# A gated unit that finishes in its PSUM tile, and block differences accumulated in two PSUM banks lent by the first ring

## The chip, the cores and the metric

The kernel runs on one core of a Trainium2 chip. Its engines work from queues of their own and meet only at semaphores: TensorE (PE in the profile; PEld are its weight loads), VectorE (DVE), ScalarE (ACT), GpSimd (POOL) and SyncE (SP), which issues most transfers. Matmul results land in PSUM, eight banks of 128 partitions x 512 fp32 words; everything else lies in SBUF. GpSimd instructions in this kernel read and write SBUF alone. The metric is the device time of one execution in microseconds (us), as the median of several runs; lower is better.

## The reference, cut to what matters

One layer of a diffusion backbone over 1024 latent tokens of width 1024, after a 256-token context prefix: a bidirectional S5 state-space mixer with a gated output, then a SwiGLU feed-forward layer with 2816 hidden units, with RMS norms and adaptive shift, scale and gate around both.

```python
def out(y, h):                       # end of the S5 mixer
    y = y.reshape(h.shape).astype(h.dtype) + d_skip * h
    g = jax.nn.gelu(y)
    return g * jax.nn.sigmoid(g @ w_glu + b_glu)
...
x = x + m_l[2][:, None] * y_l
h_l = modulate(rms_norm(x, norm_ffn[i]), m_l[3][:, None], m_l[4][:, None])     # "h2"
x = x + m_l[5][:, None] * swiglu(h_l, ffn_w1[i], ffn_w3[i], ffn_w2[i])
return rms_norm(x, norm_final)
```

All arrays are fp32. The kernel reaches that accuracy with matmuls in a rounded fp32 type: each operand is split into a rounded high part and the rest, its low part, and a product takes three matmuls (high x high, high x low, low x high).

## The kernel before

The program is written in the order in which each engine runs its own instructions. No planner moves anything: generators (`glu_unit`'s `others`, `rest`, `CNT`) say in which step of one piece of work a step of another is emitted. A PSUM tile taken from a ring of `bufs` waits, on the engine that writes it first, until the earlier holder of that bank was last used.

**The gated unit.** The latent tokens are eight rows `s` of 128; the 1024 output columns are four quarters `cq`. `glu_unit(cq, s)` is one unit, 32 in all; I number them 0 to 31 in program order: units 0 to 15 run quarter by quarter over rows 0 to 3, units 16 to 31 row by row over rows 4 to 7. A unit is 24 matmuls into a PSUM tile `pz` of 256 columns (from `pe`, a ring of eight banks), then on VectorE the bias into an SBUF tile `sg` (tile name `ru`), on ScalarE the sigmoid in place, on VectorE the product with `y` and the sum with the residual row `xs`, on ScalarE a square with its row sum, written back to `pz` as a place to drop it. That square (line 1054) is the last use of the bank. Units 0 to 7 also transpose a piece of the later rows (`gt_steps`), so each takes two banks and the matmuls of unit n+4 wait for the square of unit n. GpSimd meanwhile multiplies the rows by their gate (`gate`) and, after units 1 and 5, forms the low part of the next quarter of weights (`split`, with a ScalarE copy, line 952, and the transfer `load_glu` around it).

**h2.** During units 16 to 31 the finished rows are normed and transposed: `h2s` (GpSimd) scales a row, `h2t_steps` transposes four blocks to PSUM, applies shift and scale (`kk` 0 on ScalarE, line 1110; `kk` 1 on VectorE, line 79) into the SBUF tile `tb`, copies the high part (line 1112) and subtracts it for the low part (GpSimd for `kk` 0, VectorE for `kk` 1).

**The feed-forward layer** has 22 hidden tiles of 128. Tiles 0 and 1 take the plain product (`up_plain`, n = 0 and 1 for the two halves of the tokens); each half is four quarters of 12 matmuls (`mm4`) into two `pu` banks, the first closed by a Silu on ScalarE (line 1238), the second by a VectorE product, then `gate_up` makes high and low parts. `down` follows: 16 groups of three matmuls into the `pd` ring (four banks), each added to the result by VectorE. From tile 2 on, `up` multiplies 2x2 blocks with seven products instead of eight (Strassen and Winograd's form), which needs sums and differences of the blocks of h2. These are made once, during tiles 0 and 1: for each row `t3_steps` is three VectorE operations (rows 2 and 3: GpSimd) and `t24_steps` four, the third of `t3` and the second and fourth of `t24` followed by `t_split` (a ScalarE copy, line 1154, and a GpSimd subtraction). `CNT` puts 6 of these steps into the second half of tile 0, 12 into the first half of tile 1, 7 into its second half; the rest goes into the two `down` and, for `t1_steps`, tile 2. Tile 2's first product `mm(2, 0)` stands between tile 1 and its `down`. `load2` scales and splits a tile's rows of `w2`.

Elementwise VectorE and GpSimd operations go through one helper, so the profile shows them all at line 70; tile names tell them apart: `pe`, `pu`, `pd` are PSUM, `ru`, `rxa`, `rxc`, `ra`, `r` and `c` SBUF.

Of the kernel before, what the change touches and what calls it, by code (L numbers as in the profile page):

```python
# [10 lines left out]
F32 = mybir.dt.float32  # L11
R32 = mybir.dt.float32r
I32 = mybir.dt.int32
AF = mybir.ActivationFunctionType
# [3 lines left out]
P = 128  # L18
# [19 lines left out]
def s5_ffn_kernel(tc, a, out):  # L38
    nc = tc.nc
    V, S, E, PE, SY = nc.vector, nc.scalar, nc.gpsimd, nc.tensor, nc.sync  # L40
    ctx = ExitStack()
    with ctx:
        ctx.enter_context(tc.manual_schedule())
        sb = ctx.enter_context(tc.tile_pool(name="sb", bufs=1))
        def region(tag, kb, dt=F32):
            return sb.tile([P, int(kb * 256)], dt, tag=tag, name=tag)

        def view(reg, kb, shape, parts=P):
            off = int(round(kb * 256))
            n = int(np.prod(shape))  # L50
            v = reg[:parts, off:off + n]
            if len(shape) > 1:
                names = "abcdef"[:len(shape)]
                v = v.rearrange(f"p ({' '.join(names)}) -> p {' '.join(names)}",
                                **{k: d for k, d in zip(names, shape)})
            return v
# [3 lines left out]
        RU = region("ru", 40)  # L60
# [8 lines left out]
        def tt(o, x, y, op, eng=V):  # L69
            eng.tensor_tensor(out=o, in0=x, in1=y, op=op)  # L70
# [10 lines left out]
        MUL, ADD, SUB = OP.mult, OP.add, OP.subtract  # L81
# [3 lines left out]
        def small(shape, parts=P):  # L85
            v = view(R0, pos[0], shape, parts)
            pos[0] += int(np.prod(shape)) / 256
            assert pos[0] <= 7, pos[0]
            return v
# [16 lines left out]
        ssq, ss2, rt, rtt = small([T, 4]), small([T]), small([T]), small([T])  # L106
# [16 lines left out]
        def pw(shape=(4, P)):  # L123
            return pA.tile([P] + list(shape), F32, tag="w", name="pw", bufs=3)
# [363 lines left out]
        pt = mix_rows()  # L488
# [130 lines left out]
        for hb in range(16):  # L619
# [10 lines left out]
            elif hb == 2:  # L630
                pt = mix_rows()
# [300 lines left out]
        def gt_hi(k, half, eng=S):  # L932
            pt = pe8([4, P])
            for i in range(4):
                PE.transpose(pt[:, i], Y[:, k, 4 * half + i], ident)
            if eng is S:
                S.copy(GH[half][0][:, :, k], pt)
            else:
                eng.tensor_copy(GH[half][0][:, :, k], pt)
            return pt  # L940
# [16 lines left out]
        def gh_(s):  # L957
            h_, l_ = GH[s // 4]
            return h_[:, s % 4], l_[:, s % 4]
# [4 lines left out]
        def glu_mm(cq, s, ks):  # L964

            wH, wL = (w.rearrange("p (k n) -> p k n", k=8) for w in WR[cq])
            h_, l_ = gh_(s)
            new = (cq, s) not in PZ
            if new:
                PZ[cq, s] = [pe8([256]), 0]  # L970
            pz, n = PZ[cq, s]
            for k in ks:
                PE.matmul(pz, h_[:, k], wH[:, k], start=n == 0, stop=False)
                PE.matmul(pz, h_[:, k], wL[:, k], start=False, stop=False)
                PE.matmul(pz, l_[:, k], wH[:, k], start=False, stop=n == 7)
                n += 1
            PZ[cq, s][1] = n
            return pz
# [7 lines left out]
        bglu = view(RU, 32, [D])  # L986
        SY.dma_start(bglu, a["b_glu"].to_broadcast([P, D]))
        ps_ = {}
        for i in range(10):
# [7 lines left out]
            if i >= 3:  # L997
                pt = gt_hi(order[i - 3], 0, V if i in GHV else S)
# [29 lines left out]
        GH[1] = (view(GR, 0, [4, 8, P]), view(GR, 16, [4, 8, P]))  # L1028
        WR += [(view(GR, 32 + 16 * i, [8 * 256]), view(GR, 40 + 16 * i, [8 * 256])) for i in range(3)]
        TT = [[view(GR, 32 + 16 * i + 8 * j, [4, 4, P]) for j in range(2)] for i in range(3)]  # L1030
        sg = [view(RU, 36 + i, [256]) for i in range(2)]
        ui = [0]

        def glu_unit(cq, s, *others):

            def step():
                for g in others:
                    next(g, None)

            cs_ = slice(cq * 256, cq * 256 + 256)  # L1040
            ks = order if s < 4 else range(8)
            pz = glu_mm(cq, s, ks[PZ[cq, s][1] if (cq, s) in PZ else 0:])
            step()
            o = sg[ui[0] % 2]
            ui[0] += 1
            tt(o, pz, bglu[:, cs_], ADD)
            S.activation(o, o, AF.Sigmoid)
            step()
            y = Y[:, 2 * cq:2 * cq + 2, s]
            o = o.rearrange("p (k n) -> p k n", k=2)  # L1050
            tt(o, o, y, MUL)
            tt(y, o, xs[s % 4][:, cs_].rearrange("p (k n) -> p k n", k=2), ADD)
            step()
            S.activation(pz.rearrange("p (k n) -> p k n", k=2), y, AF.Square, accum_out=ssq[:, s, cq:cq + 1])
            step()

        def gt_steps(k):
# [41 lines left out]
        def h2t_steps(s, pool, tbs, kk):  # L1099
            h_, l_ = gh_(s)  # L1100
            pt, tb, ks = pool([4, P]), tbs[kk], slice(4 * kk, 4 * kk + 4)
            for i in range(4):
                PE.transpose(pt[:, i], tb[:, i], ident)
            yield
            for i in range(4):
                k = 4 * kk + i
                if kk:
                    ts(tb[:, i], pt[:, i], mod2[:, 1, k:k + 1], MUL, mod2[:, 0, k:k + 1], ADD)
                else:
                    S.activation(tb[:, i], pt[:, i], AF.Identity, bias=mod2[:, 0, k:k + 1], scale=mod2[:, 1, k:k + 1])  # L1110
            yield
            S.copy(h_[:, ks], tb)
            yield
            tt(l_[:, ks], tb, h_[:, ks].bitcast(F32), SUB, V if kk else E)
# [17 lines left out]
        for cq in range(4):  # L1132
            for s in range(4):
                k = 4 * cq + s
# [28 lines left out]
        for u in range(16):  # L1163
            s, cq = 4 + u // 4, u % 4
            gens = []
            if u >= 2:
                j, kk = (u - 2) // 2, u % 2
# [12 lines left out]

        psF = tc.tile_pool(name="psF", bufs=1, space=bass.MemoryType.PSUM, reuse_waits="tile")
        pF = psF.__enter__()

        def pf(shape):
            return pF.tile([P] + list(shape), F32, tag="dn", name="pd", bufs=4)

        def pu_():
            return pF.tile([P, 512], F32, tag="u", name="pu", bufs=4)

        w2raw = view(RU, 32, [D])  # L1190
        tmp = [view(r, kb + 2 * i, [512]) for r, kb in ((RU, 36), (RXa, 0)) for i in range(2)]
# [20 lines left out]
        def mm4(pu, w, b, start, stop):  # L1212
            for k in range(4):
                mm3(pu, w[0][:, k], w[1][:, k], b[0][:, :, k], b[1][:, :, k], start and k == 0, stop and k == 3)
# [8 lines left out]
        def up_plain(ft, n, rest, at={}):  # L1223
            ps_ = []
            for q in range(4):
                j = (0, 2, 1, 3)[q] if n else q
                w, i = divmod(j, 2)
                if i == 0:
                    ps_.append(pu_())
                mm4(ps_[w], OP_[ft, j], bb_(i, n), i == 0, i == 1)  # L1230
                if q in at:
                    at[q]()
                if n and (ft + 1 < NPL or j < 2):
                    op_split(ft + 1, j, raw[:, j])
                for _ in range(CNT[ft][n][q]):
                    next(rest, None)
            t = tmp[n]
            S.activation(t, ps_[0], AF.Silu)
            tt(t, ps_[1], t, MUL)
            gate_up(ft, n, t)  # L1240

# [3 lines left out]
        def bb_(i, j):  # L1245
            return [t[:, :, 4 * i:4 * i + 4] for t in GH[j]]
# [11 lines left out]

        def t3_steps(s, t, eng):
            b12, b22 = (f32s(hl(x, s)) for x in (BV[6], BV[5]))  # L1260
            tt(t, b22[0], b12[0], SUB, eng)
            yield
            tt(t, t, b22[1], ADD, eng)
            yield
            tt(t, t, b12[1], SUB, eng)
            t_split(hl(BV[3], s), t, E)
            yield

        def t24_steps(s, t3, t2, t4):
            b11, b21 = (f32s(hl(x, s)) for x in BV[:2])  # L1270
            tt(t2, t3, b11[0], ADD)
            yield
            tt(t2, t2, b11[1], ADD)
            t_split(hl(BV[2], s), t2, E)
            yield
            tt(t4, t2, b21[0], SUB)
            yield
            tt(t4, t4, b21[1], SUB)
            t_split(hl(BV[4], s), t4, E)
            yield  # L1280

# [27 lines left out]
        def mm(ft, j):  # L1309
            pu = pu_()  # L1310
            mm4(pu, OP_[ft, j], BV[j], True, True)
            return pu
# [110 lines left out]
        load2(1)  # L1423
        up_plain(1, 0, rest)
        up_plain(1, 1, rest)
        pu = mm(NPL, 0)
        down([NPL - 1], False, prep(NPL))

# [4 lines left out]
        for ft in range(NPL, NFT - 1):  # L1433
            load2(ft)
            pu = up(ft, pu, {j: t1_go for j in range(4)} if ft == NPL else {})
# [64 lines left out]
```

## Time and profile before

| | |
|---|---|
| median of 3 runs | 1121.35 us (1119.0 to 1121.96) |
| the profiled execution | 1119.82 us; span of its trace 1117.6 us |
| mean granted TensorE clock | 0.961 of full |
| TensorE busy | 1005.8 us, 90% of the span |
| VectorE, GpSimd, ScalarE busy | 821.7 us, 629.6 us, 415.1 us |
| S5 mixer, up to the gated unit | to about 308 us of the span |
| gated unit and h2 | about 308 to 420 us |
| hidden tiles 0 and 1 | about 420 to 510 us |
| hidden tiles 2 to 21, final norm | about 510 us to the end |

A group row of the profile reads: line, engine, operation, out<-in by tile names, shapes, count | busy time, mean ns of one | idle time of the engine just before them and who ended it. A timeline row reads: start, duration, engine, line, operation, and in brackets the idle time before it and its releaser. A row over windows gives for each stretch its length, then each engine's busy time with its number of instructions, the granted TensorE clock (1.00 is full), the share of the transfer engines and GB/s. A matmul's shown duration overlaps the next one's; the distance between starts is what counts.

### The profile page before, as it was taken

The numbers are of one execution on the slowest core, as the hardware profiler recorded it, in microseconds if no ns is written. First come the engines' busy times: TensorE is split into PE (matmuls) and PEld (weight loads), VectorE is DVE, ScalarE is ACT, GpSimd is POOL, SyncE is SP. The second block draws the span as 40 slices with busy tenths as digits, with TensorE's granted clock in tenths as the row PEclk, the third lists the DMA queues.
The fourth block names the chain that finished last, engine by engine and source line by source line (L and its number), as shares of the span: only waits on it lengthen the run. The fifth ranks groups of instructions, "written<-read, shape, count | busy, mean of one in ns | idle before, by whom it ended". The sixth has DMA issues, their size and how long they took to land. (4 is left out here: it accounts for less than half of the span.)

```text
span 1117.6 us, 16924 instructions
## 1 busy us (share of the span) xinstructions
PE 1005.8 (90%) x6208; PEld 807.3 (72%) x6208; DVE 821.7 (74%) x1808; ACT 415.1 (37%) x870; POOL 629.6 (56%) x484
## 2 busy tenths in 40 slices
PE   4889896637969999879999999999999999999997
PEld 1556632536869997667888888888888888888885
DVE  7688989993877787988666666666666666666657
ACT  4338731625834564232222222222222222222236
POOL 4446777980382353865655555555555555555563
PEclk9989998768999999899999999999999999999999
DMA  9577778663421201101111111111111111111114
GB/s 327 212 208 152 189 247 223 160 137 99 152 76 41 75 1 59 59 15 57 57 57 56 37 35 43 57 57 57 57 57 57 57 57 57 57 57 57 40 37 150
DMA packets 54514, 103.04 MB, mean 92 GB/s; under 512 B 4384, under 2 KB 25120, under 8 KB 53408
## 3 DMA queue, kind: packets, MB, share of 16 engines
q1 hardware_dynamic: 46656, 85.57, 23.1%
q0 software_dynamic: 3456, 12.58, 6.0%
q10 hardware_dynamic: 4320, 3.81, 1.1%
q8 instruction: 49, 0.80, 0.3%
q14 instruction: 33, 0.27, 0.1%
HBM read 83.20 MB, written 6.16 MB: 80 GB/s over the span
## 5 line engine op out<-in xcount | busy, mean ns | idle before, releaser
L70 POOL TENSOR_TENSOR c<-rxc,c 128x512 fp32r<-128x512 f32 x128 | 170.3, 1345 | 184.4 <-ACT c L1154 179.4
L70 DVE TENSOR_TENSOR ru<-pd,ru 128x512 f32<-128x512 f32 x336 | 227.0, 690 | 2.6 <-PE pd L1210 2.6
L1210 PE MATMUL pu<-ra,c 128*128 128x512 f32 x432 | 168.3, 390 | 0.6 <-POOL c L70 0.6
L1209 PE MATMUL pu<-ra,c 128*128 128x512 f32 x432 | 168.2, 389 | 0.6 <-DVE ra L70 0.6
L1208 PE MATMUL pu<-ra,c 128*128 128x512 f32 x432 | 168.3, 390 | 0.3 <-ACT ra L1154 0.3
L1154 ACT CAST c<-rxc 128x512 fp32r<-128x512 f32 x128 | 76.8, 617 | 187.5 <-POOL rxc L70 107.4
L1208 PE MATMUL pd<-c 128*128 128x512 f32 x336 | 133.3, 397 | 10.9 <-DVE ru L70 10.9
L1209 PE MATMUL pd<-c 128*128 128x512 f32 x336 | 132.6, 395 | 0.0
L1210 PE MATMUL pd<-c 128*128 128x512 f32 x336 | 132.2, 394 | 0.0
L70 DVE TENSOR_TENSOR ru<-pu,ru 128x512 f32<-128x512 f32 x84 | 57.9, 689 | 86.8 <-PE pu L1210 52.0
L70 POOL TENSOR_TENSOR c<-ru,c 128x1024 fp32r<-128x1024 f32 x22 | 53.2, 2419 | 85.7 <-ACT c L952 77.1
L1210 PEld LDWEIGHTS pu<-ra,c 128*128 128x128 f32 x432 | 81.1, 188 | 18.3 <-POOL c L70 1.4
L1209 PEld LDWEIGHTS pu<-ra,c 128*128 128x128 f32 x432 | 81.1, 188 | 17.7 <-POOL c L70 0.9
L1208 PEld LDWEIGHTS pu<-ra,c 128*128 128x128 f32 x432 | 81.1, 188 | 17.5 <-ACT ra L1154 0.8
L1208 PEld LDWEIGHTS pd<-c 128*128 128x128 f32 x336 | 64.2, 191 | 26.3 <-DVE ru L70 12.9
L1210 PE MATMUL pu<-c,c 128*128 128x512 f32 x192 | 74.8, 390 | 0.2 <-POOL c L70 0.2
L1208 PE MATMUL pu<-c,c 128*128 128x512 f32 x192 | 74.9, 390 | 0.0
L1209 PE MATMUL pu<-c,c 128*128 128x512 f32 x192 | 74.7, 389 | 0.0
L1210 PEld LDWEIGHTS pd<-c 128*128 128x128 f32 x336 | 64.2, 191 | 13.6
L1209 PEld LDWEIGHTS pd<-c 128*128 128x128 f32 x336 | 64.2, 191 | 13.2
L70 DVE TENSOR_TENSOR ru<-ru,rxa 128x512 f32<-128x512 f32 (+1 forms) x62 | 62.3, 1006 | 7.4 <-ACT ru L1353 3.5
L70 POOL TENSOR_TENSOR c<-rxc,rxa 128x1024 f32<-128x1024 f32 x30 | 62.3, 2158 | 4.5 <-PE pw L602 4.5
(320 smaller groups left out, 2230.2 us busy)
## 6 DMA issues: line engine op xcount, KB each, us to landing
ru<-in_w SPq DMA_DIRECT2D x22, 512.0 KB, 3.6
c<-in_ada_w SPq DMA_DIRECT2D x40, 256.0 KB, 4.5
rxc<-in_w SPq DMA_DIRECT2D x38, 256.0 KB, 4.6
rxc<-in_w SPq DMA_DIRECT2D x19, 512.0 KB, 5.3
c<-c POOLq DMA_DIRECT2D x18, 512.0 KB, 5.4
ra<-in_ada_w SPq DMA_DIRECT2D x24, 256.0 KB, 5.6
ra<-in_ada_w SPq DMA_DIRECT2D x10, 512.0 KB, 11.0
ru<-in_xT SPq DMA_DIRECT2D x4, 1024.0 KB, 7.8
```

The costliest lines, as they stand in the source:

```text
L70: eng.tensor_tensor(out=o, in0=x, in1=y, op=op)
L1154: S.copy(o[0], x)
L1208: PE.matmul(pu, wh, bh, start=start, stop=False)
L1209: PE.matmul(pu, wh, bl, start=False, stop=False)
L1210: PE.matmul(pu, wl, bh, start=False, stop=stop)
```

## The change

1. In `glu_unit` the SBUF tiles `sg` are gone. Bias, sigmoid and product are written in place into `pz`; the sum with `xs` reads `pz` and writes `y` as before. The square goes to the same tile as before.
2. In `h2t_steps` the half `kk` 1 applies shift and scale in place in the PSUM tile of its transposes; the copy of the high part and the subtraction read that tile.
3. `t3_steps` (on VectorE) and `t24_steps` take a tile `pt` of 512 columns in PSUM. ScalarE copies the first block into it, VectorE accumulates the next block or blocks there, and the last operation of each chain reads it and writes the SBUF tile as before. These are ten new ScalarE copies.
4. The pool for tiles 0 and 1 has four `pd`, two `pu` (four before) and two `pt`. Behind tile 1's second half it is closed and one with four `pd` and four `pu` is opened.
5. In `up_plain` the Silu is emitted as soon as the first `pu` is full (after quarter 1 of half 0, quarter 2 of half 1), not behind the half.

```diff
@@ glu_unit
             pz = glu_mm(cq, s, ks[PZ[cq, s][1] if (cq, s) in PZ else 0:])
             step()
-            o = sg[ui[0] % 2]
-            ui[0] += 1
-            tt(o, pz, bglu[:, cs_], ADD)
-            S.activation(o, o, AF.Sigmoid)
+            tt(pz, pz, bglu[:, cs_], ADD)
+            S.activation(pz, pz, AF.Sigmoid)
             step()
             y = Y[:, 2 * cq:2 * cq + 2, s]
-            o = o.rearrange("p (k n) -> p k n", k=2)
+            o = pz.rearrange("p (k n) -> p k n", k=2)
             tt(o, o, y, MUL)
             tt(y, o, xs[s % 4][:, cs_].rearrange("p (k n) -> p k n", k=2), ADD)
             step()
-            S.activation(pz.rearrange("p (k n) -> p k n", k=2), y, AF.Square, accum_out=ssq[:, s, cq:cq + 1])
+            S.activation(o, y, AF.Square, accum_out=ssq[:, s, cq:cq + 1])
@@ h2t_steps
             yield
+            if kk:
+                tb = pt
             for i in range(4):
@@ the pool of tiles 0 and 1
+        NPU = [2]
         def pu_():
-            return pF.tile([P, 512], F32, tag="u", name="pu", bufs=4)
+            return pF.tile([P, 512], F32, tag="u", name="pu", bufs=NPU[0])
+
+        def pt_():
+            return pF.tile([P, 512], F32, tag="t", name="pt", bufs=2)
@@ up_plain
                 mm4(ps_[w], OP_[ft, j], bb_(i, n), i == 0, i == 1)
+                if q == 1 + n:
+                    t = tmp[n]
+                    S.activation(t, ps_[0], AF.Silu)
                 if q in at:
...
-            t = tmp[n]
-            S.activation(t, ps_[0], AF.Silu)
             tt(t, ps_[1], t, MUL)
@@ t3_steps
-            tt(t, b22[0], b12[0], SUB, eng)
-            yield
-            tt(t, t, b22[1], ADD, eng)
-            yield
-            tt(t, t, b12[1], SUB, eng)
+            a_ = t
+            if eng is V:
+                a_ = pt_()
+                S.copy(a_, b12[0])
+            tt(a_, b22[0], b12[0] if a_ is t else a_, SUB, eng)
+            yield
+            tt(a_, a_, b22[1], ADD, eng)
+            yield
+            tt(t, a_, b12[1], SUB, eng)
             t_split(hl(BV[3], s), t, E)
@@ t24_steps
-            tt(t2, t3, b11[0], ADD)
-            yield
-            tt(t2, t2, b11[1], ADD)
+            a_ = pt_()
+            S.copy(a_, b11[0])
+            tt(a_, t3, a_, ADD)
+            yield
+            tt(t2, a_, b11[1], ADD)
             t_split(hl(BV[2], s), t2, E)
             yield
-            tt(t4, t2, b21[0], SUB)
-            yield
-            tt(t4, t4, b21[1], SUB)
+            a_ = pt_()
+            S.copy(a_, b21[0])
+            tt(a_, t2, a_, SUB)
+            yield
+            tt(t4, a_, b21[1], SUB)
             t_split(hl(BV[4], s), t4, E)
@@ between tile 1 and mm(2, 0)
         up_plain(1, 1, rest)
+        psF.__exit__(None, None, None)
+        psF = tc.tile_pool(name="psG", bufs=1, space=bass.MemoryType.PSUM, reuse_waits="tile")
+        pF = psF.__enter__()
+        NPU[0] = 4
         pu = mm(NPL, 0)
```

Two places in the order of the engines' instructions. VectorE at unit 0, first before and then as changed (the first two rows lie ahead of the unit; in the next three `pe` is the unit's PSUM tile, `ru` the bias, the old SBUF tile and `y`, `c_3168` the residual row; the last row is of `gt_steps`):

```order
L70 TENSOR_TENSOR c_2975<-pe,c_2974 128x4x128 x3
L70 TENSOR_TENSOR ra<-rxc,ra 128x2048
L70 TENSOR_TENSOR ru<-pe,ru 128x256
L70 TENSOR_TENSOR ru<-ru 128x256
L70 TENSOR_TENSOR ru<-ru,c_3168 128x2x128
L70 TENSOR_TENSOR ra<-pe,ra 128x4x128
```

```order
L70 TENSOR_TENSOR c_2975<-pe,c_2974 128x4x128 x3
L70 TENSOR_TENSOR ra<-rxc,ra 128x2048
L70 TENSOR_TENSOR pe<-pe,ru 128x256 x2
L70 TENSOR_TENSOR ru<-pe,c_3168 128x2x128
L70 TENSOR_TENSOR ra<-pe,ra 128x4x128
```

Bias, product and sum keep their places (bias and product read alike now and share the row marked x2), but product and sum have one PSUM and one SBUF input where both lay in SBUF.

ScalarE in the first half of tile 1, first before and then as changed (`ru<-pu` is the Silu, `ra<-rxa` and `ra<-r_60` the copies of `t_split`, `c_4432<-ru` the copy of `gate_up`; the `pt` rows are the new copies):

```order
L952 CAST c_4432<-ru 128x1024
L1154 CAST ra<-rxa 128x512 x2
L1154 CAST ra<-r_60 128x512
L1154 CAST ra<-rxa 128x512 x2
L1238 ACTIVATE ru<-pu 128x512
L1219 CAST c_4432<-ru 128x512
```

```order
L952 CAST c_4432<-ru 128x1024
L1266 COPY pt<-ra 128x512
L1151 CAST ra<-rxa 128x512
L1234 ACTIVATE ru<-pu 128x512
L1278 COPY pt<-c_2974 128x512
L1151 CAST ra<-rxa 128x512
L1285 COPY pt<-c_2974 128x512
L1151 CAST ra<-r_60 128x512
L1278 COPY pt<-c_2974 128x512
L1151 CAST ra<-rxa 128x512
L1285 COPY pt<-c_2974 128x512
```

The Silu stands further ahead, and each new copy stands behind the `t_split` copy of the chain before it, whose input is that chain's last VectorE operation; the next chain's first VectorE operation reads what the new copy writes.

More of the change, by code (lines that the diff above doesn't have):

```diff
@@ L1030, in s5_ffn_kernel @@
         TT = [[view(GR, 32 + 16 * i + 8 * j, [4, 4, P]) for j in range(2)] for i in range(3)]
-        sg = [view(RU, 36 + i, [256]) for i in range(2)]
-        ui = [0]
         def glu_unit(cq, s, *others):
```

## Prediction

> **What bounds the kernel now.** I read the totals, then busy time by stage (PE, PEld, DVE, ACT, POOL, then the granted clock), then what TensorE waits for.
>
> ```profile
> PE 1005.8 (90%) x6208; PEld 807.3 (72%) x6208; DVE 821.7 (74%) x1808; ACT 415.1 (37%) x870; POOL 629.6 (56%) x484
> ...
> 310.22:341.77 31.55, 22.55 (x171) 21.84 (x170) 25.63 (x26) 11.64 (x27) 21.82 (x8) 0.89 0.20 68
> 341.77:420.27 78.50, 76.24 (x635) 75.23 (x634) 63.15 (x141) 38.98 (x113) 33.60 (x25) 1.00 0.13 41
> ...
> 447.26:466.08 18.82, 13.90 (x50) 10.49 (x49) 17.02 (x21) 3.80 (x7) 16.58 (x13) 0.82 0.22 80
> 466.08:491.10 25.02, 24.77 (x110) 20.19 (x109) 23.16 (x20) 7.05 (x11) 15.87 (x11) 1.00 0.07 22
> 491.10:510.54 19.44, 13.41 (x49) 10.56 (x48) 17.16 (x22) 4.02 (x7) 13.07 (x10) 0.82 0.00 0
> 527.00:1085.00 558.00, 557.58 (x2459) 461.03 (x2458) 365.72 (x518) 149.49 (x246) 313.02 (x228) 1.00 0.16 52
> ```
>
> The borders are first matmuls of stages: units 2 to 7; units 8 to 31; (tile 0 up left out); tile 0's `down`; tile 1 up with mm(2, 0); its `down`; steady tiles. In the last row TensorE is busy 557.6 of 558 us at full clock, so nothing gained on VectorE there shortens it. The room lies in the rows above: 9.0 us idle in the first, 2.3, 4.9, 0.3 and 6.0 in the next four, and a clock under 0.9 in three of them. Who ends TensorE's waits there:
>
> ```profile
> PE pd L1208 <- DVE ru L70: 10.9, 2, 6.0
> PE pe L973 <- ACT pe L1054: 9.0, 3, 6.2
> PE pe L1103 <- POOL rxa L70: 2.3, 5, 0.9
> PE pd L1103 <- DVE rxa L77: 2.2, 1, 2.2
> ```
>
> ScalarE's square at 1054 is late only because VectorE is late, so three of the four are VectorE's. The longest of them in time order (VectorE, GpSimd, TensorE):
>
> ```profile
> 326.10 3.99 DVE L70 TENSOR_TENSOR ru<-ru 128x256 f32<-128x256 f32 x1 [2.37 <-ACT ru L1047]
> 330.13 2.44 DVE L70 TENSOR_TENSOR ru<-ru,c 128x256 f32<-128x256 f32 x1
> ...
> 325.28 4.53 POOL L70 TENSOR_TENSOR ra<-rxc,ra 128x2048 fp32r<-128x2048 f32 x1 [2.76 <-ACT ra L952]
> ...
> 333.23 0.58 PE L973 MATMUL pe<-ra,c 128*128 128x256 f32 x1 [6.20 <-ACT pe L1054]
> ```
>
> The product of 256 columns ends 0.28 us behind the GpSimd instruction that began before it: it waited for it whole. Groups of 308 to 345 us, then 345 to 420, show which forms suffer:
>
> ```profile
> L70 DVE TENSOR_TENSOR ru<-ru 128x256 f32<-128x256 f32 x7 | 12.7, 1812 | 7.4 <-ACT ru L1047 7.4
> ...
> L70 DVE TENSOR_TENSOR ru<-pe,ru 128x256 f32<-128x256 f32 x7 | 2.9, 411 | 0.0
> ...
> L70 DVE TENSOR_TENSOR ru<-ru,c 128x256 f32<-128x256 f32 x24 | 18.9, 785 | 0.8
> L70 DVE TENSOR_TENSOR ru<-ru 128x256 f32<-128x256 f32 x24 | 16.3, 679 | 11.8 <-ACT ru L1047 11.8
> ```
>
> Two SBUF inputs cost 0.68 to 1.81 us on average, one PSUM input 0.41 under the same GpSimd load.
>
> **The change, part by part.** First, the price of an operation that writes PSUM (groups of the S5 mixer, where such tiles exist):
>
> ```profile
> L70 DVE TENSOR_TENSOR ltb<-ra,lta 128x256 f32<-128x256 f32 x17 | 7.2, 426 | 3.3 <-ACT ra L521 1.8 <-ACT ltb L684 1.2
> L70 DVE TENSOR_TENSOR lta<-ra,lta 128x64 f32<-128x64 f32 x96 | 21.2, 220 | 0.2
> L696 ACT COPY kt<-r 128x480 f32<-128x480 f32 x1 | 0.5, 548 | 0.0
> ```
>
> PSUM and SBUF in, PSUM out is 0.43 us at 256 columns, and with input and output in one bank (second row) no dearer in kind. I take 0.42 for product and sum; bounds 0.41 and, for the unshown in-place form at this width, twice that. A copy of 512 columns into PSUM I take at 0.57, scaled from 0.548 for 480.
>
> *Units 0 to 7.* Undisturbed, a unit costs TensorE the distance of two transposes:
>
> ```profile
> 313.18 0.60 PE L935 MATMUL pe<-r,ru 128*128 128x128 f32 x4
> 316.49 0.60 PE L935 MATMUL pe<-r,ru 128*128 128x128 f32 x4
> ...
> 341.42 0.60 PE L935 MATMUL pe<-r,ru 128*128 128x128 f32 x4
> ```
>
> 3.31 us. Units 4 to 7 took 24.93 where 13.24 would do: 11.7 lost, 9.0 waiting and the rest at half clock. VectorE's unit becomes 3 x 0.42, 0.5 for the sigmoid and 0.68 for the low part: 2.4 us, under 3.31. What is late next is a transfer that ScalarE's queue meets:
>
> ```profile
> 312.72 0.38 SPq L1019 DMA_DIRECT2D rxc<-in_w_glu  x1
> ...
> rxc<-in_w_glu SPq DMA_DIRECT2D x2, 1024.0 KB, 5.1
> ...
> L952 ACT CAST ra<-rxc 128x2048 fp32r<-128x2048 f32 x3 | 5.7, 1900 | 0.0
> ```
>
> The copy behind unit 1 (line 952) cannot start before 312.7 + 5.1 = 317.8 and takes 1.9, one of 0.6 follows, so unit 2's sigmoid starts at 320.3; its product, sum and square end at 322.2, and unit 6's matmuls need them at 316.85 + 2 x 3.31 = 323.5. The copy behind unit 5 meets a transfer that GpSimd's subtraction releases at about 325.5 (gates to 321, then the 4.53): it lands at 330.6, and ScalarE's queue stands until 332.5. Units 8 to 11 take one bank each, and unit 12 needs unit 6's square (about 335) only at 342. So nothing, with 7 us to spare. **-11.7 us**; bounds -7 (the 1.3 us margin at unit 6 gone, and at 7 too) and -11.7.
>
> *Units 16 to 31.*
>
> ```profile
> L79 DVE TENSOR_SCALAR rxa<-pe,r 128x128 f32<-128x128 f32 x24 | 8.2, 401 | 0.3
> L70 DVE TENSOR_TENSOR c<-rxa,c 128x512 fp32r<-128x512 f32 x4 | 4.4, 1102 | 0.0
> ```
>
> The 0.3 us waits of h2's transposes follow VectorE's lag (POOL's subtraction waits for ScalarE, which stands behind a late sigmoid). Over two units VectorE drops from about 6.5 us (2 x 0.42, 0.68 + 0.79 twice, four operations of 0.40, one of 1.10) and a sigmoid's wait of 0.5 to 6 x 0.42 + 1.6 + 0.69 = 4.8 and that wait, in TensorE's 2 x 3.31 = 6.6. **-1.9** of the 2.3; bounds 0 and -2.3. The 2.2 us on line 77, where unit 31's norm chain is late, goes the same way: the last four units save 0.63 each and a low part 0.4, some 2.9 us. **-2.2**, bounds -1 and -2.2.
>
> The Trainium skill, "VectorE: DVE Perf Modes", section "Rules for kernel authors", speaks against all this: for elementwise work on a matmul's output it says to copy PSUM to SBUF first if many operations follow, and the page's cycle table (its section on the TRN2 errata) has 62 more fixed cycles for a PSUM source. That would be an estimated 65 ns for each of two operations in 32 units: 4 us on VectorE, within the slack above, and a word for the rival called slower below. This trace disagrees: 411 ns with a PSUM input against 679 or more without, since GpSimd is at work beside it.
>
> *Tile 0.* Its block differences and pd groups, before:
>
> ```profile
> 454.30 0.68 DVE L70 TENSOR_TENSOR ru<-pd,ru 128x512 f32<-128x512 f32 x1
> ...
> 455.04 0.80 PE L1208 MATMUL pd<-c 128*128 128x512 f32 x1 [4.90 <-DVE ru L70]
> ...
> 437.13 1.28 ACT L1238 ACT_TABLE_LOAD   x1
> ...
> 443.26 1.13 ACT L1154 CAST c<-rxc 128x512 fp32r<-128x512 f32 x2
> ...
> 440.44 0.69 DVE L70 TENSOR_TENSOR c<-ru,c 128x512 fp32r<-128x512 f32 x1 [0.69 <-ACT c L1219]
> ```
>
> The fifth pd group waits for the first's sum, 18.0 us after the second half of the up product began (four quarters of 2.75 ahead of 447.26: 436.26). Now the Silu is early: the table load of 1.28, the Silu and the first product of some 0.6 each leave the chain ahead of `gate_up` and lie under matmuls, so `load2`'s product is done 2.6 us sooner, and behind two ScalarE copies the one into `pt` ends at 5.5 us of the half. A chain of two VectorE operations takes 0.73 + 0.69 (0.04 between them, as at 330.13); then `t_split`'s copy (0.51 to the next start, from 1.13 for two) and the new copy (0.57) with two handovers of 0.04: 1.16 in which VectorE waits if nothing else is due. So t3 ends at 7.75, the first chain of t24 at 10.3, its third operation at 12.2, the product at 12.9, the low part (two SBUF inputs, 1.4 again) at 15.0, the first pd sum at 15.7. The fifth group waits 2.0 instead of 4.9, too short for the half clock (18.82 - 11.0 - 4.9 = 2.9 us here; the waits of 4.9, 6.0 and 6.2 have it, the stages with 2.2 and less do not), and the sixth 0.65 for the one difference between. 18.82 becomes 11.0 + 2.65: **-5.2**; bounds -2 and -7.9 (no wait at all).
>
> *Tile 1.* Here the ring of two `pu` decides. T is the start of its first half. Before:
>
> ```profile
> 485.41 0.69 DVE L70 TENSOR_TENSOR ru<-pu,ru 128x512 f32<-128x512 f32 x1 [0.59 <-ACT ru L1238]
> ...
> 500.01 0.79 PE L1208 MATMUL pd<-c 128*128 128x512 f32 x1 [6.03 <-DVE ru L70]
> ...
> L70 DVE TENSOR_TENSOR rxa<-rxa,c 128x512 f32<-128x512 f32 x6 | 8.0, 1339 | 0.3
> ...
> 466.88 2.25 DVE L70 TENSOR_TENSOR ru<-ru,rxa 128x1024 f32<-128x1024 f32 x1
> ...
> 499.00:505.00 6.00, 4.99 (x12) 3.94 (x13) 4.76 (x8) 1.14 (x2) 5.19 (x4) 0.51 0.00 0
> ```
>
> 108 matmuls in 24.77 us make a quarter 2.75. The product at T+19.3 (466.08 to 485.41) emptied the second `pu` with no one waiting; TensorE ran to the fifth pd group and waited 6.0 there, then had half clock (0.51): 19.44 - 11.0 - 6.0 = 2.4 more. Now quarter 1 of the second half needs that bank at T+13.75, and behind it on TensorE stand the rest of the half, mm(2, 0) and `down`. VectorE: four pd sums to T+2.1, `load2`'s product to 4.5 (2.25 again, behind GpSimd), two ScalarE copies, t3 from 6.7 to 8.8, three ScalarE instructions, t24's first chain 10.5 to 11.9; three more chains at 1.42 + 1.16 = 2.58 to 19.6, one copy and one operation to 21.5, product to 22.2. A pair of differences thus takes 2.58 where two at 1.34 took 2.68: the gain per operation is spent on waiting for ScalarE. TensorE waits 8.4 us, loses some 1.0 at half clock (less than 2.4, since more of that state passes in the longer wait), then needs 3 x 2.75 + 2.75 + 11.0; VectorE has seven differences, two products and two low parts more (about 12 us, to T+34.5), done when `down` has just begun, so the 6.0 there is gone. End at T+45.1 against 44.46: **+0.6**; bounds -7 (the copies run ahead and the bank comes at T+15) and +6 (each chain 1 us longer).
>
> Sum: 11.7 + 1.9 + 2.2 + 5.2 - 0.6 = 20.4 off the profiled execution's 1119.8 gives 1099.4; the median lies 1.5 higher, 1100.9. I say 1100.
>
> **The rivals.** *ScalarE's chain costs more* (0.14): its copies queue behind `op_split`'s, which wait for TensorE to free a weight slot. For it: one queue holds both. Against: in the walk above the new copies' inputs are always later than those slots. At 1 us a chain +5 in tile 1 and +2 in tile 0: 1107. *The ring of two does no harm* (0.08): chains without the wait end at T+15 and tile 1 gains 7: 1093. The order shown speaks against it, since the new copy stands behind the old one. *Nothing is freed* (0.04): a VectorE operation with one SBUF input still waits for GpSimd when it also writes PSUM. Time 1120. The 0.41 with a PSUM input and the 426 above, in a kernel whose GpSimd is 56% busy, are against. *Slower* (0.05): reading and writing one PSUM bank costs double. Per pair of units 2 biases, 2 products and 4 shift-and-scales are in place; VectorE has 6.6 - 4.8 - 0.5 = 1.3 us of slack, so from 0.16 us each TensorE pays; at +0.42, 2 us in each of eight pairs, the 4.1 of the lead-in not regained, +2 and +4 in tiles 0 and 1: 1120 - 20.4 + 26 = 1125. The 220 for 64 columns in place speaks against.
>
> **How the numbers follow.** Forecast 0.69, own range 1095 to 1105. All bounds at once give 1089 and 1116; the range is 1092 to 1110, which takes in the first two rivals and the bounds that can fall together. About 0.3% is what a measurement of this kernel can tell from no change: faster 0.91, same 0.04, slower 0.05.
>
> **What would show it.** Right: units 0 to 7 at 3.31 us; `ru<-pe,c` at 0.42; no wait of line 973 on 1054; one wait of some 8 us of `pu` on VectorE in tile 1's second half and none at its `down`; about 2 us at tile 0's. Wrong: a wait for `pt`, in-place rows above 0.5 us, or a steady stage that is no longer full.

## The result and the profile after

| | before | as changed |
|---|---|---|
| median | 1121.35 us | 1101.32 us (1099.35 to 1101.53, five runs) |
| ratio of the medians | 1 | 0.9823, 95% interval 0.9806 to 0.9841 |
| profiled execution, its span | 1119.82 us, 1117.6 us | 1099.35 us, 1097.1 us |
| mean granted TensorE clock | 0.961 | 0.969 |

The change takes 20 us off, 1.8%. The totals of the changed kernel (busy time of each engine) and its stages, at the borders that the prediction used (units 2 to 7; units 8 to 31; tile 0 up; tile 0's `down`; tile 1 up with mm(2, 0); its `down`; steady tiles; in each row the span, then busy time of PE, PEld, DVE, ACT and POOL, the granted clock, and the transfers):

```profile
PE 1000.6 (91%) x6208; PEld 803.8 (73%) x6208; DVE 777.2 (71%) x1808; ACT 419.2 (38%) x880; POOL 621.8 (57%) x484
```

```profile
311.20:331.09 19.89, 19.89 (x172) 19.89 (x170) 13.59 (x26) 10.51 (x26) 19.89 (x8) 1.00 0.28 91
331.09:406.27 75.18, 75.18 (x635) 75.18 (x634) 50.42 (x146) 41.81 (x120) 33.52 (x26) 1.00 0.15 47
406.27:430.87 24.60, 24.60 (x124) 20.73 (x123) 14.50 (x36) 14.56 (x29) 10.59 (x9) 1.00 0.24 86
430.87:444.22 13.35, 11.50 (x50) 8.86 (x48) 12.30 (x19) 2.75 (x5) 9.98 (x9) 1.00 0.24 79
444.22:479.23 35.01, 26.09 (x109) 21.17 (x108) 18.99 (x26) 13.20 (x23) 22.68 (x17) 0.90 0.05 16
479.23:490.11 10.88, 10.88 (x49) 9.01 (x48) 10.34 (x16) 1.14 (x2) 6.58 (x5) 1.00 0.00 0
...
507.00:1065.00 558.00, 557.52 (x2457) 460.87 (x2456) 367.51 (x518) 149.53 (x247) 312.29 (x227) 1.00 0.16 52
```

Against the rows of before: 31.55 became 19.89 (-11.7), 78.50 became 75.18 (-3.3), 26.99 became 24.60 (-2.4), 18.82 became 13.35 (-5.5), and tile 1 with its `down`, 44.46, became 45.89 (+1.4). That sums to -21.4. The part ahead of the units was 1.0 longer in this execution (the border row that stood at 310.22 stands at 311.20), which leaves about the 20.5 between the spans. In the first three rows TensorE is now busy for the whole stretch at full clock, so no wait is left to remove there; the steady tiles are what they were. Of the long waits one is left in these stages, and it is new (TensorE's waits between 308 and 490 us, sum, count, longest):

```profile
PE pu L1209 <- DVE ru L70: 8.9, 1, 8.9
PE pd L1209 <- DVE ru L70: 1.9, 2, 1.6
```

Bias, product and sum of a unit, in the stretch of units 2 to 7 (groups by form):

```profile
L70 DVE TENSOR_TENSOR pe<-pe,ru 128x256 f32<-128x256 f32 x13 | 5.6, 427 | 5.5 <-ACT pe L1042 5.5
...
L70 DVE TENSOR_TENSOR ru<-pe,c 128x256 f32<-128x256 f32 x6 | 2.5, 424 | 0.2
```

All three take 0.42 to 0.43 us, where the product took 1.81, and GpSimd is busy beside them all through the stretch (19.89 us in the first row). The PSUM form is not quicker in itself: where GpSimd was idle in the kernel before, the product with two SBUF inputs took as little:

```profile
336.99 0.42 DVE L70 TENSOR_TENSOR ru<-ru 128x256 f32<-128x256 f32 x1 [0.51 <-ACT ru L1047]
```

### The profile page after: what moved, and what is told of

It is laid out like the page before. It is cut to its first block, busy times and chain, and to the rows that moved or that the text cites. A ratio compares the mean times of both kernels' runs of the same rounds, so it can differ in the third digit from the quotient of the medians.

```text
span 1097.1 us, 16934 instructions
## 1 busy us (share of the span) xinstructions
PE 1000.6 (91%) x6208; PEld 803.8 (73%) x6208; DVE 777.2 (71%) x1808; ACT 419.2 (38%) x880; POOL 621.8 (57%) x484
## 4 chain that ended last, share of the span: by engine, by line
PE 74%; DMA 6%; ACT 6%; DVE 6%; POOL 5%; issue 2%; ACTq 0%; SPq 0%; POOLq 0%; DVEq 0%
PE pu L1211 11%; PE pu L1210 11%; PE pu L1209 11%; PE pd L1209 7%; PE pd L1211 7%; PE pd L1210 7%; PE pw L516 3%; PE pe L974 3%; PE pe L975 3%; PE pe L973 3%; POOL c L70 3%; DVE ru L70 2%; PE prow L282 2%; DMA rxc<-in_cxy 1%; PE pm L470 1%
## 5 line engine op out<-in xcount | busy, mean ns | idle before, releaser
L70 POOL TENSOR_TENSOR c<-rxc,c 128x512 fp32r<-128x512 f32 x128 | 166.9, 1319 | 186.9 <-ACT c L1151 179.8
L1209 PE MATMUL pd<-c 128*128 128x512 f32 x336 | 131.1, 390 | 1.9 <-DVE ru L70 1.9
L1211 PE MATMUL pd<-c 128*128 128x512 f32 x336 | 130.7, 389 | 0.0
L1210 PE MATMUL pd<-c 128*128 128x512 f32 x336 | 130.7, 389 | 0.0
L1209 PEld LDWEIGHTS pd<-c 128*128 128x128 f32 x336 | 63.1, 188 | 16.1 <-DVE ru L70 3.1
L1211 PEld LDWEIGHTS pd<-c 128*128 128x128 f32 x336 | 63.1, 188 | 13.1
L1210 PEld LDWEIGHTS pd<-c 128*128 128x128 f32 x336 | 63.1, 188 | 12.9
L952 ACT CAST c<-ru 128x1024 fp32r<-128x1024 f32 x21 | 22.1, 1050 | 112.8 <-DVE ru L70 112.8
```

What stands on the lines that cost most here:

```text
L952: S.copy(hl[0], raw)
L1209: PE.matmul(pu, wh, bh, start=start, stop=False)
L1210: PE.matmul(pu, wh, bl, start=False, stop=False)
L1211: PE.matmul(pu, wl, bh, start=False, stop=stop)
```

## The experiments

Seven more kernels, and the changed kernel once more. Each is told by the same five stretches (the kernel with GpSimd's work in pieces only in its own section); tile 1 stands with mm(2, 0) and its `down`. "After" is the first profile of the changed kernel; the last rows are ratios to the kernel before, from runs on the same chip as each.

| us | before | after | units alone | tiles alone | no `pt` | ring 3 and 3 | copies ahead | ahead, no part 2 |
|---|---|---|---|---|---|---|---|---|
| units 2 to 7 | 31.55 | 19.89 | 19.88 | 32.03 | 19.88 | 19.88 | 19.88 | 19.88 |
| units 8 to 31 | 78.50 | 75.18 | 75.18 | 78.48 | 75.18 | 75.19 | 75.19 | 75.19 |
| tile 0 up | 26.99 | 24.60 | 24.60 | 26.98 | 24.59 | 24.59 | 24.59 | 24.59 |
| tile 0 down | 18.82 | 13.35 | 19.16 | 13.37 | 15.41 | 14.04 | 12.13 | 12.13 |
| tile 1 | 44.46 | 45.89 | 44.47 | 46.95 | 43.82 | 44.22 | 36.01 | 35.94 |
| ratio | 1 | 0.9823 | 0.9842 | 0.9975 | 0.9805 | 0.9808 | 0.9715 | 0.9711 |
| 95% from | | 0.9806 | 0.9812 | 0.9958 | 0.9781 | 0.9783 | 0.9689 | 0.9687 |
| to | | 0.9841 | 0.9872 | 0.9992 | 0.9830 | 0.9834 | 0.9741 | 0.9735 |

The stretches repeat to some hundredths where nothing waits, while the work ahead of the units ends up to 5 us earlier or later from one execution to the next (units 2 to 7 begin at 306 to 311 us). So a part's price is read from its stretch, and the total is the check on it.

### Is it the length of GpSimd's instructions?

The theory is that a VectorE operation with two SBUF inputs waits for the running GpSimd instruction as a whole. If so, the cure needs no PSUM: GpSimd's work in shorter pieces must do as well.

```diff
 (the kernel before; the low part of a quarter of weights, and the gates)
-            tt(hl[1], raw, hl[0].bitcast(F32), SUB, eng)
+            m = 256 if eng is E and raw.shape[-1] == 2048 else raw.shape[-1]
+            for i in range(0, raw.shape[-1], m):
+                p = slice(i, i + m)
+                tt(hl[1][:, p], raw[:, p], hl[0][:, p].bitcast(F32), SUB, eng)
...
         def gate(s, ks):
+            (one instruction for each row and 256 columns)
```

> The kernel before, with GpSimd's work during units 0 to 7 cut into instructions of 256 columns: the low part of a quarter of weights as eight instructions in place of one of 2048 columns, the gates as pieces of 256 columns; the same elements are computed, nothing of VectorE's is changed. Theory (a VectorE operation with two SBUF inputs waits for the running GpSimd instruction as a whole): no wait is longer than one piece, some 0.6 us, so the product and sum of a unit go from 1.81 and more to 0.5 to 1.0 us in the mean, TensorE's 9.0 us of waits on the square fall to 0 to 3, and the time by 6 to 12 us, 1109 to 1115. Rival (the two engines share the SBUF path element by element, so that the length of an instruction doesn't matter): the mean stays within 0.2 us of 1.81 and the time within 2 us of the kernel before, or above it by the fixed cost of the added instructions.

Measured: 1113.35 us, 6.6 under the kernel before, ratio 0.9947 (0.9925 to 0.9969). The groups of VectorE and GpSimd from 306 to 328 us, then the stretches of units 2 to 7, units 8 to 31 and tile 0 up:

```profile
L70 DVE TENSOR_TENSOR ru<-ru 128x256 f32<-128x256 f32 x6 | 4.4, 732 | 5.0 <-ACT ru L1050 5.0
...
L70 POOL TENSOR_TENSOR ru<-ru,rxa 128x256 f32<-128x256 f32 x19 | 16.4, 900 | 0.0
L70 POOL TENSOR_TENSOR ra<-rxc,ra 128x256 fp32r<-128x256 f32 x8 | 6.3, 826 | 0.0
```

```profile
308.06:327.93 19.87, 19.87 (x171) 19.87 (x169) 14.74 (x22) 10.18 (x24) 19.87 (x24) 1.00 0.16 54
327.93:410.20 82.27, 78.41 (x635) 76.88 (x634) 62.41 (x145) 40.54 (x115) 42.41 (x44) 0.98 0.16 52
410.20:438.77 28.57, 26.40 (x123) 21.92 (x122) 19.71 (x40) 14.13 (x30) 9.45 (x6) 0.94 0.17 58
```

The product went from 1.81 to 0.73 us with VectorE's program untouched, TensorE's 9.0 us of waits are gone, and units 2 to 7 take 19.87 us, as in the changed kernel. The rival (the two share the path element by element) falls. The single instructions say the same. Between 306 and 345 us, eight products and sums of the kernel before and 18 of this one start while a GpSimd instruction runs, and every one ends 0.28 to 0.29 us behind that instruction's end, whether it then took 4.15 us or 0.44. The Trainium skill, "SBUF — State Buffer", section "Who interferes with whom", states it as these rows and those of the changed units show it: an instruction of VectorE with two SBUF inputs contends with a GpSimd instruction that reads SBUF, one with at most one SBUF input doesn't (outside that engine's two-port modes).

The same profile shows what the PSUM form is better at. Eight pieces of 256 columns take 6.3 us on GpSimd where one instruction took 4.53, so the last quarter's low part comes late: TensorE waits 1.7 us for it and runs at half clock after, and units 8 to 31 give back 3.8 of the 11.7 us. The 1.6 us of the last stretch have another cause. The kernel before has the same wait of 2.2 us there (line 77), but kept its full clock, while here half clock followed it. The same stretch before, and the wait here:

```profile
420.27:447.26 26.99, 24.82 (x124) 20.65 (x123) 19.91 (x40) 14.04 (x30) 9.45 (x6) 1.00 0.18 62
```

```profile
420.81 1.48 PE L1114 MATMUL pd<-r,rxa 128*128 128x128 f32 x8 [2.17 <-DVE rxa L77]
```

### The unit alone, and the tiles alone

The kernel before with part 1 only (the unit in its PSUM tile, the diff's first part), and with parts 3 to 5 only (`pt`, the pools, the early Silu):

> The kernel before with part 1 alone: bias, sigmoid and product of a gated unit in its PSUM tile. Theory (the two-SBUF-input operations are what waits for GpSimd, in the unit itself): units 2 to 7 go from 31.55 us to 19.6 to 20.1, no wait of TensorE on the square is left, units 8 to 31 lose 1 to 2 of their 78.5 us, the 2.2 us wait on line 77 ahead of tile 0 shrinks to 0 to 1.2; the waits of 4.9 and 6.0 us at the two downs stay. In all -14 to -16 us, 1105 to 1107. Rival (the gain of units 16 to 31 and of line 77 belongs to part 2, the h2 half in PSUM): -12 us, 1109, units 8 to 31 at 78 to 78.5 and the 2.2 us wait still there.

> The kernel before with parts 3, 4 and 5 alone: block differences in two PSUM tiles, four pd, two pu, early Silu. Theory: tile 0's down goes from 18.8 to 13 to 14 us, tile 1 with mm(2, 0) and its down stays within -1 to +2 of 44.5 with one wait of 8 to 9 us on pu in the place of the 6.0 us at down; the units stay as before. In all -4 to -5.5 us, 1116 to 1117.5. Rival (these parts only do well behind a faster unit stage, since their copies queue behind late work there): within 2 us of the kernel before.

Measured: the unit alone 1101.02 us, ratio 0.9842 (0.9812 to 0.9872); the tiles alone 1117.77 us, 0.9975 (0.9958 to 0.9992). Stretches of the unit alone (units 2 to 7, 8 to 31, tile 0 up) and its waits of TensorE from 308 to 490 us:

```profile
306.20:326.08 19.88, 19.88 (x172) 19.88 (x170) 13.58 (x26) 10.51 (x26) 19.88 (x8) 1.00 0.27 91
326.08:401.26 75.18, 75.18 (x635) 75.18 (x634) 50.41 (x145) 41.43 (x118) 33.02 (x26) 1.00 0.16 48
401.26:425.86 24.60, 24.60 (x124) 20.73 (x123) 16.87 (x36) 12.46 (x26) 8.73 (x6) 1.00 0.20 67
```

```profile
PE pd L1203 <- DVE ru L70: 10.9, 2, 6.0
```

The three stretches are those of the changed kernel to 0.01 us, without part 2. So all of their 17.4 us is part 1's, and the two `down` keep their 4.9 and 6.0. The median's 18.9 less agrees with -17.0 for the five rows of the table within its interval (-14 to -21). That is more than the 14 to 16 I had expected: units 8 to 31 gave 3.3 and not 1 to 2, and the wait on line 77 is gone altogether. The rival, that part 2 has a share of it, falls. The tiles alone gave -5.45 at tile 0's `down` and +2.5 at tile 1, -2.2 us in all by the medians, where -4 to -5.5 was expected: with 0.5 lost again in the untouched units 2 to 7; the wait on `pu` was the expected one (8.9 us), but the half clock behind it lasted longer. The rival here (these parts only do well behind a faster unit stage) falls by tile 0's `down`: 13.37 us behind the old units, 13.35 behind the new. Two profiles of the changed kernel itself show how much that half clock varies with nothing changed, since it was run once more:

> The changed kernel itself, to have it on one chip beside the three below: 0.980 to 0.984 of the kernel before.

Its median was 1098.97 us, 0.9819 (0.9792 to 0.9847), the same result. After the same wait (8.92 and 8.96 us), stretches of 1 us from where TensorE resumes, in the first profile and in this one:

```profile
466.90:467.90 1.00, 1.00 (x2) 0.83 (x3) 0.37 (x1) 1.00 (x2) 0.00 (x0) 0.50 0.00 0
...
468.90:469.90 1.00, 1.00 (x4) 0.78 (x3) 0.00 (x0) 1.00 (x2) 0.82 (x2) 0.58 0.00 0
469.90:470.90 1.00, 1.00 (x6) 0.81 (x5) 0.87 (x2) 0.06 (x1) 0.94 (x1) 1.00 0.00 0
```

```profile
468.62:469.62 1.00, 0.99 (x2) 0.83 (x3) 0.37 (x1) 1.00 (x2) 0.00 (x0) 0.50 0.00 0
...
472.62:473.62 1.00, 1.00 (x4) 0.79 (x3) 1.00 (x2) 0.45 (x1) 0.00 (x0) 0.50 0.00 0
473.62:474.62 1.00, 1.00 (x6) 0.83 (x5) 0.93 (x3) 0.17 (x1) 0.75 (x1) 0.98 0.00 0
```

Half clock for 2.8 us in one, 5.0 in the other: tile 1 and its `down` took 45.89 and 46.98 us. The tiles alone had 5.0 too.

### What does `pt` bring as it stands?

The changed kernel without part 3 and without the pools of part 4, so four `pu` and four `pd` throughout:

```diff
-            a_ = pt_()
-            S.copy(a_, b11[0])
-            tt(a_, t3, a_, ADD)
+            tt(t2, t3, b11[0], ADD)
             yield
-            tt(t2, a_, b11[1], ADD)
+            tt(t2, t2, b11[1], ADD)
 (the same for the other chains; no psG)
```

> The changed kernel without part 3: the block differences in SBUF by VectorE alone as before, no copies into pt, four pu and four pd throughout; units, h2 and the early Silu as changed. Theory by the prediction's walk (the early Silu takes 2.6 us out of VectorE's chain ahead of tile 0's fifth pd group, the rest of that gain is the differences'): tile 0's down 15 to 16.5 us (13.35 as changed, 18.82 before), tile 1 with down 44 to 45 (45.9 as changed): 0 to +2 us against the changed kernel. Rival 1 (the Silu's place does nothing, since VectorE stands on the differences anyway): tile 0's down stays at 18 to 19, +3.5 to +5. Rival 2 (all of tile 0's gain is the Silu's): 13 to 13.5, -1.5 to -1.

Measured: 1097.97 us, ratio 0.9805 (0.9781 to 0.9830), beside 0.9819 for the changed kernel in the same comparison: no difference that these runs can tell. Tile 0's `down`:

```profile
429.38:444.79 15.41, 12.78 (x49) 9.62 (x48) 14.38 (x19) 2.82 (x5) 13.20 (x10) 0.89 0.20 68
```

The early Silu alone brings tile 0's `down` from 19.16 (the unit alone) to 15.41. The wait of its fifth group falls from 4.9 to 2.2 us, as the prediction's walk (its step-by-step timing) had it, though some half clock stays behind it (0.89 in the stage). `pt` brings 2.06 more there and costs 2.1 to 3.2 in tile 1 (43.82 against 45.89 and 46.98). So as it stands part 3, with its pools, pays nothing, and possibly costs 1 us.

### Ring or chain?

Two readings of the 8.9 us wait: the ring of two `pu` is too short, or VectorE comes too late because each chain of two differences waits for ScalarE. The chain, in the changed kernel, on VectorE and on ScalarE (start, duration, engine, line, operation, idle time before it and its releaser):

```profile
457.50 0.70 DVE L70 TENSOR_TENSOR pt<-rxa,pt 128x512 f32<-128x512 f32 x1 [1.18 <-ACT pt L1285]
458.30 0.69 DVE L70 TENSOR_TENSOR r<-pt,c 128x512 f32<-128x512 f32 x1
460.23 0.70 DVE L70 TENSOR_TENSOR pt<-r,pt 128x512 f32<-128x512 f32 x1 [1.24 <-ACT pt L1278]
```

```profile
448.85 0.62 ACT L1151 CAST ra<-r 128x512 fp32r<-128x512 f32 x1 [6.25 <-POOL r L70]
...
450.33 0.58 ACT L1266 COPY pt<-ra 128x512 f32<-128x512 f32 x1
...
459.02 0.62 ACT L1151 CAST ra<-r 128x512 fp32r<-128x512 f32 x1 [1.56 <-DVE r L70]
459.54 0.58 ACT L1278 COPY pt<-c 128x512 f32<-128x512 f32 x1
```

This chain takes 2.73 us (457.50 to 460.23; its neighbours take 2.66): VectorE's two operations, then ScalarE's copy of the result and only behind it the copy that the next chain starts from. Nor is that copy's input late: it is a block of h2 that was finished before tile 1 began. The first `pt` copy of tile 1 (450.33) stood behind a copy for which ScalarE had waited 6.25 us on GpSimd. The first experiment moves the copies, the second the ring.

```diff
 (copies one chain ahead: SRC lists the first block of each chain in order)
+        def fetch():
+            if SRC:
+                PT.append(pt_())
+                S.copy(PT[-1], b0(*SRC.pop(0)))
...
-            a_ = pt_()
-            S.copy(a_, b11[0])
+            a_ = PT.pop(0)
             tt(a_, t3, a_, ADD)
             yield
+            fetch()
             tt(t2, a_, b11[1], ADD)
             t_split(hl(BV[2], s), t2, E)
```

> The changed kernel with each of the new ScalarE copies issued one chain earlier, ahead of the t_split copy of the chain before, so that the next chain's first block lies in PSUM when VectorE comes. Theory (the chain VectorE - t_split copy - new copy - VectorE is what makes the 8.9 us wait in tile 1, not the ring of two itself): a chain of two operations falls from about 2.7 to 1.4 to 1.6 us on VectorE, the wait of 8.9 us in tile 1 falls under 1 us, the half clock behind it goes with it, and the waits of 1.62 and 0.23 us at tile 0's down go to about 0: tile 1 with down from 45.9 to 35.5 to 37, in all -9 to -12 us against the changed kernel, 1089 to 1092. Rival (VectorE is late in tile 1 anyway, since GpSimd's low parts and the reuse of the difference tiles set the pace, or the wait goes to down): the wait on pu shrinks by less than half or another of 4 us or more appears, -5 to 0 us, 1096 to 1101.

```diff
 (ring 3 and 3: the first pool)
-            return pF.tile([P] + list(shape), F32, tag="dn", name="pd", bufs=4)
+            return pF.tile([P] + list(shape), F32, tag="dn", name="pd", bufs=NPD[0])
...
-        NPU = [2]
+        NPU = [3]
+        NPD = [3]
...
-        NPU[0] = 4
+        NPU[0] = NPD[0] = 4
```

> The changed kernel with three pu and three pd instead of two and four in the first pool (two pt as before; four of each behind it). Theory (VectorE's late order is what costs, the ring of two only shows it): the 8.9 us wait on pu in tile 1 goes, TensorE runs on into its down, and waits 5 to 8 us there for a pd sum that stands behind the same differences on VectorE; tile 1 with down 43 to 47.5 against 45.9, tile 0's down 0 to 1 us longer: -3 to +2 us against the changed kernel. Rival (the ring of two is the cost of the change in tile 1): the wait goes and none comes in its place, -7 to -10 us.

Measured: copies ahead 1087.55 us, ratio 0.9715 (0.9689 to 0.9741); ring of three 1098.38 us, 0.9808 (0.9783 to 0.9834). Copies ahead, tile 0's `down`, tile 1 and its `down`, and TensorE's waits from 306 to 474 us:

```profile
425.67:437.80 12.13, 11.48 (x49) 8.85 (x48) 11.24 (x18) 2.95 (x5) 10.45 (x9) 1.00 0.24 86
437.80:462.93 25.13, 24.82 (x109) 20.20 (x108) 20.27 (x26) 12.77 (x22) 22.88 (x16) 1.00 0.07 22
462.93:473.81 10.88, 10.88 (x49) 9.01 (x48) 10.88 (x16) 1.15 (x2) 7.14 (x6) 1.00 0.00 0
```

```profile
PE pd L1209 <- DVE ru L70: 0.6, 2, 0.4
PE pu L1209 <- DVE ru L70: 0.3, 1, 0.3
```

With the ring still at two, the wait of 8.9 us is 0.3, and tile 1 takes 25.13 us where 24.7 is its matmuls alone. With its `down` it takes 36.0, inside the 35.5 to 37 that I expected; the time is 1.5 us under the 1089 to 1092. VectorE's chains in that run:

```profile
446.14 0.70 DVE L70 TENSOR_TENSOR pt<-rxa,pt 128x512 f32<-128x512 f32 x1
446.94 0.69 DVE L70 TENSOR_TENSOR r<-pt,c 128x512 f32<-128x512 f32 x1
447.55 0.69 DVE L70 TENSOR_TENSOR pt<-r,pt 128x512 f32<-128x512 f32 x1
```

1.41 us from one chain to the next here, between 1.4 and 1.6 elsewhere in the row. Ring of three, tile 1 and its `down`, and its waits from 431 to 489 us:

```profile
444.26:477.30 33.04, 27.21 (x110) 21.98 (x108) 20.13 (x26) 13.20 (x23) 22.16 (x16) 0.90 0.05 17
477.30:488.48 11.18, 11.18 (x50) 9.21 (x48) 11.17 (x16) 1.15 (x2) 7.33 (x6) 0.98 0.00 0
```

```profile
PE pu L1210 <- ACT ru L1235: 5.8, 1, 5.8
PE pd L1210 <- DVE ru L70: 2.5, 2, 2.3
```

The wait left the half and came back one product later: mm(2, 0) takes a bank that the second half's Silu frees, and that Silu stands behind two more chains in ScalarE's queue. I had expected it at `down`, on a pd sum; the place was wrong, that it only moves was right, and the stages together are 1 to 2 us shorter than the changed kernel's (58.26 against 59.24 and 60.31), not 7 to 10. So the chain through ScalarE is the cause, and the ring only decides who sees it.

### The fastest version, with part 2 undone

Copies ahead, and `h2t_steps` as before the change (`if kk: tb = pt` left out):

> The copies one chain ahead as in the run before, with part 2 undone: shift and scale of h2's second half written to SBUF again. Theory (part 2 does nothing: without the waits of the units VectorE has time for the dearer low part): units 8 to 31 at 75.2 us, no wait on line 77 or on h2's transposes, tile 1 with down 36 us, -10 to -13 us against the changed kernel. Rival (part 2 is what removed the 0.3 us waits and the 2.2 us on line 77 once the copies are ahead): units 8 to 31 at 76 to 78 and 1 to 2 us of wait ahead of tile 0, -7 to -10.

Measured: 1087.45 us, ratio 0.9711 (0.9687 to 0.9735), the same as with part 2. Units 8 to 31 and tile 0 up:

```profile
330.44:405.63 75.19, 75.19 (x636) 75.19 (x634) 50.41 (x145) 41.29 (x118) 33.00 (x26) 1.00 0.15 48
405.63:430.22 24.59, 24.59 (x124) 20.73 (x122) 16.06 (x38) 15.41 (x32) 11.51 (x9) 1.00 0.25 86
```

TensorE is full in both, so part 2 brings nothing that can be seen, whether the copies are ahead or not. Both versions with the copies ahead beat the kernel before (by 2.9%) and the changed one (0.9711 against 0.9819 in one comparison, 11.5 us between the medians).

## Why the prediction was right

Forecast 1100 us, measured 1101.32. The mechanism held in every stage, but that the spans fit to 0.1 us (20.4 forecast, 20.5 measured) is luck: the stages gave 1.0 us more than forecast, and the part ahead of them, which the change doesn't touch, took 1.0 longer in this execution. The steps one by one:

- **Units 0 to 7**: -11.7 predicted, -11.7 measured, and the mechanism holds by its own test (GpSimd in pieces gives the same stretch). The transfer that ScalarE's queue meets cost TensorE nothing, as the walk had it.
- **Units 8 to 31**: -1.9 predicted with -2.3 as the bound, -3.3 measured. The bound counted only the idle time shown. Transposes of h2 in the kernel before, undisturbed and with such a wait:

```profile
380.15 0.60 PE L1103 MATMUL pe<-r,rxa 128*128 128x128 f32 x4
383.46 0.60 PE L1103 MATMUL pe<-r,rxa 128*128 128x128 f32 x4
387.26 0.66 PE L1103 MATMUL pe<-r,rxa 128*128 128x128 f32 x4 [0.33 <-POOL rxa L70]
```

  A wait shown as 0.33 us lengthened the distance from 3.31 to 3.80. The prediction also gave part of the gain to part 2 (the low part at 0.69 where 1.10 stood, which it does cost now); the unit alone gave all of it.
- **Lead-in to tile 0**: -2.2 predicted, -2.4 measured.
- **Tile 0**: -5.2 predicted, -5.5 measured, the waits 1.6 and 0.2 against 2.0 and 0.65. The walk's share of the early Silu (2.6 us off the wait) was right as well: without `pt` the wait is 2.7 us shorter. That such a short wait would bring no half clock held here (clock 1.00), but the prediction's reason, that waits of 2.2 us and less don't have it, did not: 2.2 us without `pt` had it, and 2.2 us ahead of tile 0 with GpSimd in pieces. So that part of the term was luck.
- **Tile 1**: +0.6 predicted, +1.4 and +2.5 measured in the two profiles. The wait was at the place and of the size named (8.4 against 8.9), and the 6.0 at `down` is gone. Two things in the walk were off. The half clock behind the wait was put at 1.0 us, "since more of that state passes in the longer wait"; it cost 1.4 and 2.4. And t3 began at T+6.7 as said, but not because `load2`'s product takes 2.25 us: that took 1.27, and VectorE then stood 4.6 us on a `pt` copy that ScalarE's queue held behind GpSimd's last operation of another row:

```profile
450.94 0.69 DVE L70 TENSOR_TENSOR pt<-ra,pt 128x512 f32<-128x512 f32 x1 [4.64 <-ACT pt L1266]
```

  The two errors cancelled, so that start, and with it much of the 8.4, was right by luck.

Of the rivals, "the ring of two does no harm" was wrong for this change, but its mechanism, the copies running ahead, is what the fastest version does on purpose: 36.0 us in tile 1, where the prediction's bound was 7 us under 44.5 and the run went 8.5 under. "ScalarE's chain costs more" came out in a small way (2.66 to 2.73 against 2.58), and its queue showed where the walk had not looked, in the 4.6 us. "Slower", doubled cost in place, did not: 0.43 us at 256 columns and 0.70 at 512, where the old bias took 0.41 and a sum from PSUM to SBUF 0.68. "Nothing is freed" falls by the same rows. Of the signs of being wrong, a wait for `pt` did show in part: no copy waited for a bank, but VectorE waited ten times for a copy, 16.8 us in all from 425 to 490 us, where the walk had about 1.2 for each chain. What the prediction did not see is that its own sentence on the chains ("the gain per operation is spent on waiting for ScalarE") names a loss that a different place of ten copies removes: 11 us in the two tiles (12.13 + 36.01 against 13.35 + 45.89), more than twice what the change itself gained there.

## What to carry to other kernels

Where VectorE and GpSimd work side by side, look first at the groups with two SBUF inputs: if their mean is far over the smallest one, see whether each ends just behind a GpSimd instruction. Here it did, and moving one operand to PSUM (or cutting GpSimd's instruction, at a price on GpSimd) gave that back. A copy that only prepares an operand belongs in its engine's queue ahead of anything that waits for the chain it feeds; behind it, the queue turned two engines into one chain. The longer ring did not cure the late producer here, it moved the wait to the next taker of a bank.

## What the runs showed of the hardware

- After the same wait of 8.9 us TensorE ran at half clock for 2.8 us in one execution and for 5.0 in two others, a difference of 1.1 us in the stage. The Trainium skill, "TensorE: Matmul & The Clock Gate", section "What's actually happening", has the clock set by a free-running window of some 3.4 us, so that the end of the slow state depends on where in the window the work resumes. That the length varies agrees; the variation it gives, half a microsecond to either side, is less than these runs show.
- The length of a wait alone did not decide whether half clock followed: 2.2 us ahead of tile 0 had none in the kernel before (1.00 in the stage) and had it with GpSimd in pieces (0.94); at tile 0's `down`, 2.3 us with the ring of three had none (1.00), 2.2 us without `pt` had it (0.89). What decides stays open.
- Accumulating in place in PSUM cost hardly more than from PSUM to SBUF: 427 ns for `pe<-pe,ru` beside 424 for `ru<-pe,c` and 411 for the old bias, all under GpSimd's load.
- GpSimd paid for short instructions: where VectorE did not meet them, pieces of 256 columns followed each other every 0.70 us, where an eighth of the 2048-column instruction would be 0.57. The mean of 0.83 in the row above also holds pieces of 0.92 us, which began while a product or sum was under way on VectorE.
